# A list scheduler's order, tiled products and the conv half of the output projection inside the scan of a bidirectional RWKV-7 layer

## The chip, the cores and the metric

The kernel runs on one core of one Trainium2 chip. The metric is the device time of one execution in microseconds; a lower one is better. The times shown are three runs of the kernel before; the profile is one execution, recorded by the hardware profiler.

## What is computed

One layer of a bidirectional diffusion backbone, for 128 context tokens and 2048 latent tokens of width 1024. All is f32. Cut to what matters:

```python
h = rmsnorm(x) * (1 + scale) + shift
r, k, v, g_a, b_gate, c_gate, u_conv, g_b = split(h @ w_in)
r, k, v = token_shift(r, k, v)
ya = wkv(h, r, k, v, s0) * silu(g_a)          # 512 channels, 8 heads of 64, two directions
yb = b_gate * conv3(c_gate * u_conv) * silu(g_b)   # 512 channels
u = concat([ya, yb]) @ w_out
y = rmsnorm(x + gate * u) * final_g
# in wkv, per head and direction, for each token t:
S = S * w_t - (S @ kk_t) (kk_t * a_t)^T + v_t k_t^T
out_t = S @ r_t
```

## The kernel before

The work stands in three phases. **Phase 1** computes the norm, the input projection, the shifts, decays and the conv group, and spills them to DRAM scratch: `ops0` and `ops1` (four operands for each direction), `vt`, `sg`, `q`, and `mixT`, in whose rows 512 to 1023 the conv half `yb` lies when phase 1 ends. At its end `K.early()` begins the matrices of the first scan stages.

**Phase 2** is the scan in chunks of 64 tokens. It has 17 stages (`NST`). A stage handles a pair of heads (two heads of 64 make 128 rows) and eight chunks ("units") of each direction; stage 15 is the context, with all heads. What a stage s does, by the helper that issues it:

- `partL` loads the operands `rr` (512 KB a DMA, two for each direction); `partM` makes the matrices F and GA (`product`, L892): the operand is first copied by ACT into block-diagonal weights `bd` (`make_bd`, L779), a product uses all 128 rows and columns, DVE masks the result (L893). `transposes` makes Q (psQ, L885). The diagonal blocks of GA go to DRAM (`at`).
- `partI` runs on POOL: it loads the blocks as `ab`, inverts 32x32 triangles by substitution (L923 to L934) and stores `zt` (L935). `partM` and `partI` work on stage s+3 (`LA = 3`), in one of three slots.
- `partW` loads the stacked operands `stl`, `str` of stage s+1 (L843, L846), the values `sv` (L822), the inverse `zc` (L978); `partU` forms the inverse of 64x64 blocks from those of 32 by 32x32 products (psU L992, psW L999) into `zb`.
- `partB` makes X = F zb (L1018) and, from the stacked operands, E (L1029, masked by DVE at L1030).
- `partS` is the recurrence itself: for each of eight steps and each direction two products of E with `sv` (psS, L1054), whose upper 64 rows DVE scales into the next unit's `sv` (L1067); the lower rows are outputs, summed over directions in `y`.
- `finish` normalises a block of 512 tokens for a head pair (L1115 to L1137: square, reduce, root, scale, transposes psT L1132, gate), and stores it into `mixT` rows 0 to 511 (L1141).

All products of phase 2 are f32; the trace shows two matmul records for each.

The order of the work is written out by hand: `ORDER` and `MORD` say which piece of `partW`, `partU`, `partB` and `partM` is issued between which steps of `partS` (`main`, L1159 to L1225). Each engine works through its instructions in the order of issue; SP's queue issues nearly all DMAs.

**Phase 3** is the output projection with residual, gate and final norm, in 17 tiles of 128 tokens (`TILES`) and two column halves of 512. f32 operands are divided into two parts in f32r (`hi`, `lo`), and three products stand for one. A half of a tile needs 12 products with the attention rows (`psu<-..mha/mla`) and 12 with the conv rows (`..mhc/mlc`), L1287 to L1289. The first three tiles have their conv part done `ahead`, in stages 14 to 16 (psa); `tail` does the rest. A tile's result is multiplied by the gate (L1346), x is added (POOL, L1350), squared (L1351), scaled (L1356) and stored (L1357).

Of the kernel before, what the change touches and what calls it, by code (L numbers as in the profile page):

```python
# [672 lines left out]
SCR = {}  # L673
# [8 lines left out]
MORD = ("Ff", "GgD", "", "Q")  # L682
ON_DVE = ""
LA = 3


ORDER_END = ('LbbbL', 'UU', 'U', '', 'BBB', '', '', '', '')
ORDER = ('LbbbL', '', 'U', 'U', 'U', '', 'BBB', '', '')


def phase2(K):
# [6 lines left out]
    O.scaled = None  # L698

    def setup_first():  # L700
# [4 lines left out]
        O.pm = Pool(K, "p2m", "right", 2, PSUM)  # L705
# [15 lines left out]
        B.bd = ring(O.r1, 2, [128, 8, 128], "bd", zero)  # L721
        B.rr = ring(O.r1, 2, [128, 5, 8, 64], "rr", presetR)

    def new_slot(pool):
        i = len(B.slots)
        B.slots.append([tuple(pool.tile([128, 8, w], F32, tag=f"{n}{i}{d}", name=f"{n}{i}{d}", bufs=1) for n, w in (("F", 128), ("GA", 128), ("Q", 64))) for d in range(2)])

    def spare(i, name, dt):

        tags = ["F10", "GA10", "F11", "GA11", "F00", "F01", "GA00", "GA01"]  # L730
        if i >= 8:
            return O.rI.tile([128, 1024], dt, tag="ab", name=name, bufs=2)
        return O.r0.tile([128, 1024], dt, tag=tags[i], name=name, bufs=1)

    def setup_rest():
        O.l0 = Pool(K, "p2l0", "left")
        O.l1 = Pool(K, "p2l1", "left")
        O.p2 = Pool(K, "p2s", "left", 2, PSUM)
        O.pS = Pool(K, "p2S", "left", 4, PSUM)
# [13 lines left out]
        lt = ring(O.l1, 2, [128, 2, 8, 128], "stl", lambda t_: presetS(vl(t_)))  # L753
        rt = ring(O.l1, 2, [128, 2, 2, 8, 64], "str", presetS)
        B.lt, B.rt = lambda: vl(lt()), rt
        B.bu = O.l1.tile([128, 16, 32], F32, name="bu")
        B.zb = O.l1.tile([128, 2, 8, 128], F32, name="zb")
        zero(B.zb)

    def ring(pool, n, shape, name, init=None):  # L760
        l = [pool.tile(shape, F32, name=f"{name}{i}") for i in range(n)]
        if init:
            for t_ in l:
                init(t_)
        st = [0]

        def get():
            st[0] += 1
            return l[(st[0] - 1) % n]
        return get  # L770

    def copy(k, dst, src, negate=False):
        if negate:
            if k in ON_DVE:
                V.tensor_scalar(dst, src, -1.0, None, ALU.mult)
            else:
                P.activation(dst, src, AF.Copy, scale=-1.0)  # L777
        else:
            (V.tensor_copy if k in ON_DVE else P.copy)(dst, src)  # L779

    def zero(t_):
        G.memset(t_[:], 0.0)

    i2b = lambda n: B.I2[:].unsqueeze(1).broadcast_to((128, n, 64))

    def presetR(t_):
        V.tensor_copy(t_[:, 2], i2b(8))

    def vl(t_):
        return t_[:].rearrange("p h u (b t) -> p b h u t", b=2)  # L790

    def presetS(t_):
        for hd in range(2):
            V.tensor_copy(t_[0:64, 0, hd], B.I2[0:64].unsqueeze(1).broadcast_to((64, 8, 64)))

    def tl(shape, tag, b, pool=None, dt=F32):
        return (pool or O.l0).tile(shape, dt, tag=tag, name=f"{tag}_{K.u()}", bufs=b)

# [28 lines left out]
    H0, H1, FULL = slice(0, 64), slice(64, 128), slice(0, 128)  # L827
# [5 lines left out]
    def load_stk(t_, g, k, us):  # L833

        units = g.units[us]
        p, c0 = units[0]
        src = S[f"ops{g.d}"][k]
        n = 4 if p == units[-1][0] else 2
        for i in range(4 // n):
            dst = t_[0:64, 1, :, us.start + n * i:us.start + n * (i + 1)]  # L840
            x = src[(p + i) * 128:(p + i + 1) * 128, c0 * 64:(c0 + n) * 64]
            if t_ is g.rt:
# [5 lines left out]
    def half(g, n):  # L848

        h = n if g.d == 0 else 1 - n  # L850
        return slice(h * 4, h * 4 + 4)

    def partL(s):
        st = Ctx()
        st.g = []
        for gi, (d, units, blk) in enumerate(stages[s]):
            g = Ctx()
            st.g.append(g)
            g.d, g.units, g.blk = d, units, blk
            g.rr = B.rr()  # L860
            if blk is None:
                for i, k in ((0, 0), (1, 1), (3, 2), (4, 3)):
                    load(g.rr[:, i], d, k, units, FULL)
            else:
                p, c0 = units[0]
                src = S[f"ops{d}"][:, p * 128:(p + 1) * 128, c0 * 64:(c0 + 8) * 64]
                for i, k in ((0, 0), (3, 2)):
                    D(g.rr[:, i:i + 2].rearrange("p k u t -> p k (u t)"), src[k:k + 2].rearrange("k p t -> p k t"))
        return st

    def partM(s, st):

        at = S["at"][s]
        for gi, g in enumerate(st.g):
            d = g.d
# [28 lines left out]
            for piece in MORD:  # L904
                for c in piece:
                    ops[c]()
# [507 lines left out]
```

## Time and profile before

| | us |
|---|---|
| runs | 1751.56, 1760.31, 1761.01 |
| median | 1760.31 |
| span of the profiled execution, first to last instruction | 1752.9 |
| its PE busy | 1647.9 (94%) |
| its DVE, ACT, POOL busy | 1093.0, 870.1, 582.1 |
| first and last product of the recurrence (psS) | 1034.2, 1588.3 |
| last product of the tail | 1745.0 |

The profile gives the span of its execution and no other time for it; the median of the runs lies 7.4 us above that span, the lowest run 1.3 us below. PE is TensorE's matmuls, PEld its weight loads, DVE VectorE, ACT ScalarE, POOL GpSimd, SP the queue that issues DMAs. `L1054` is a line of the kernel. In a row of the timeline stand the start, the length, the engine, the line, the operation, output and inputs, and in the end how many records were merged; in brackets is the idle time ahead of it and what ended it. Matmuls overlap in the records, so that the time from one start to the next says what one costs, not its length. A row of groups gives busy time and mean length in ns.

### The profile page before, as it was taken

The page shows a single profiled execution, that of the slowest core. Times are in us where ns is not written, and L with a number is a line of the kernel's source. Part 1 is how long each engine was busy: PE and PEld are TensorE (multiplying, and loading weights), DVE is VectorE, ACT ScalarE, POOL GpSimd, SP SyncE. Part 2 cuts the span into 40 slices and gives each one's busy share as a digit, 9 for nine tenths or more (in the row PEclk, how much of TensorE's full clock was granted, in tenths as well). Part 3 has the DMA queues.
Part 4 walks back from the last instruction along what each step waited for, and adds up shares of the span by engine and source line. Part 5 has one row for each costly group of instructions (what it writes and reads, how often), then busy time and mean ns, then how long its engine had stood idle before and what let it go on. Part 6 is the DMA issues. An engine that isn't in the chain of part 4 may idle for free. (4 is left out here: it accounts for less than half of the span.)

```text
span 1752.9 us, 33041 instructions
## 1 busy us (share of the span) xinstructions
PE 1647.9 (94%) x12400; PEld 1558.8 (89%) x12400; DVE 1093.0 (62%) x2092; ACT 870.1 (50%) x1719; POOL 582.1 (33%) x1089
## 2 busy tenths in 40 slices
PE   5999899998999999999998989999999999899998
PEld 2889898998999998999998979899999999787886
DVE  5875788866567766567764544475776666656333
ACT  4534455534143433334442367687788787633222
POOL 0011111111011101011120587777777778223221
PEclk9899999999999999999999998899999999999999
DMA  9797778785557646477666585587677875746442
GB/s 367 208 234 220 233 241 246 232 255 151 148 160 227 169 147 174 135 258 217 195 214 225 173 196 135 141 192 187 174 198 189 191 185 120 180 151 206 151 144 90
DMA packets 315825, 335.69 MB, mean 192 GB/s; under 512 B 166985, under 2 KB 263881, under 8 KB 301585
## 3 DMA queue, kind: packets, MB, share of 16 engines
q1 hardware_dynamic: 243360, 324.52, 62.6%
q10 hardware_dynamic: 70944, 4.60, 2.9%
q0 software_dynamic: 1360, 4.46, 0.7%
q8 instruction: 98, 1.61, 0.4%
q14 instruction: 63, 0.51, 0.1%
HBM read 221.42 MB, written 112.08 MB: 190 GB/s over the span
## 5 line engine op out<-in xcount | busy, mean ns | idle before, releaser
L934 POOL TENSOR_TENSOR zt<-zt,ztmp 128x30 f32<-128x30 f32 (+7 forms) x510 | 197.3, 387 | 39.3
L1054 PE MATMUL psS<-sv,E 128*128 128x64 f32 x1088 | 155.1, 277 | 1.0 <-DVE sv L1067 0.6
L1029 PE MATMUL psE<-str,stl 128*128 128x128 f32 x1088 | 144.1, 281 | 11.3 <-DVE E L1030 7.0
L1054 PEld LDWEIGHTS psS<-sv,E 128*128 128x128 f32 x1088 | 145.4, 200 | 3.3 <-DVE sv L1067 0.8
L1029 PEld LDWEIGHTS psE<-str,stl 128*128 128x128 f32 x1088 | 131.8, 194 | 14.1 <-DVE E L1030 7.9
L931 POOL TENSOR_TENSOR ztmp<-ab,zt 128x60 f32<-128x60 f32 (+7 forms) x255 | 130.8, 513 | 19.2
L1067 DVE TENSOR_TENSOR sv<-psS,pc 64x128 f32<-64x128 f32 x254 | 69.2, 277 | 92.9 <-PE psS L1054 92.2
L779 ACT COPY bd<-rr 64x512 f32<-64x512 f32 x136 | 84.0, 617 | 75.7 <-DMA rr<-scr_ops 23.3
L323 POOL TENSOR_TENSOR shk<-rawl 128x384 f32<-128x384 f32 (+1 forms) x24 | 20.7, 861 | 291.9 <-ACT rawl L319 291.9
L1030 DVE TENSOR_TENSOR E<-psE,msk 128x512 f32<-128x512 f32 x136 | 92.7, 684 | 33.0 <-PE psE L1029 32.3
L892 PE MATMUL psF<-rr,bd 128*128 128x128 f32 x544 | 80.0, 295 | 16.2 <-ACT Q L779 9.8
L892 PEld LDWEIGHTS psF<-rr,bd 128*128 128x128 f32 x544 | 70.7, 203 | 20.4 <-ACT Q L779 12.9
L1350 POOL TENSOR_TENSOR z<-z,x 128x512 f32<-128x512 f32 x32 | 43.6, 1364 | 126.6 <-DVE z L1346 105.9
L1018 PE MATMUL psX<-F,zb 128*128 128x128 f32 x544 | 78.2, 297 | 3.2 <-ACT zb L777 2.3
L197 POOL TENSOR_TENSOR hslb<-kd,hshb 128x384 fp32r<-128x384 f32 (+1 forms) x24 | 26.7, 1113 | 164.0 <-ACT hshb L196 143.5
L160 PE MATMUL mmc<-h,w 128*128 128x384 f32 (+1 forms) x192 | 67.9, 354 | 13.4 <-ACT q1r L321 9.8
L323 POOL TENSOR_TENSOR shv<-rawl 128x384 f32<-128x384 f32 (+1 forms) x24 | 25.4, 1060 | 153.4 <-ACT rawl L319 153.4
L892 PE MATMUL psG<-rr,bd 128*128 128x128 f32 x544 | 72.0, 280 | 4.4 <-DVE F L893 4.4
L1018 PEld LDWEIGHTS psX<-F,zb 128*128 128x128 f32 x544 | 71.6, 209 | 4.0 <-POOL zt L934 1.9
L892 PEld LDWEIGHTS psG<-rr,bd 128*128 128x128 f32 x544 | 65.7, 193 | 5.0 <-DVE F L893 4.8
L161 PE MATMUL mmc<-h,w 128*128 128x384 f32 (+1 forms) x192 | 66.1, 344 | 0.0
L162 PE MATMUL mmc<-h,w 128*128 128x384 f32 (+1 forms) x192 | 65.7, 342 | 0.0
(307 smaller groups left out, 5205.4 us busy)
## 6 DMA issues: line engine op xcount, KB each, us to landing
w<-scr_wsp SPq DMA_DIRECT2D x68, 1024.0 KB, 7.3
scr_wsp<-w SPq DMA_DIRECT2D x34, 1024.0 KB, 6.0
rr<-scr_ops SPq DMA_DIRECT2D x64, 512.0 KB, 4.6
scr_ops<-sp SPq DMA_DIRECT2D x160, 192.0 KB, 5.2
wr<-in_win SPq DMA_DIRECT2D x34, 512.0 KB, 6.3
ab<-scr_at SPq DMA_DIRECT2D x34, 256.0 KB, 4.2
x<-in_x SPq DMA_DIRECT2D x17, 512.0 KB, 3.8
wadas<-in_wada SPq DMA_DIRECT2D x8, 1024.0 KB, 13.0
```

The costliest lines, as they stand in the source:

```text
L160: T.matmul(ps[:, :n], w[:, 0, k], hh[:, 0, k, :n], start=k == 0, stop=False)
L161: T.matmul(ps[:, :n], w[:, 0, k], hh[:, 1, k, :n], start=False, stop=False)
L162: T.matmul(ps[:, :n], w[:, 1, k], hh[:, 0, k, :n], start=False, stop=k == 7)
L779: (V.tensor_copy if k in ON_DVE else P.copy)(dst, src)
L892: T.matmul(ps[:, i, :].rearrange("p (a b) -> p a b", b=64), w[:, u, :], x[:, :, u, :], start=True, stop=True)
L931: G.tensor_tensor(tv, ab[:, j:j + 2, j + 2:32].unsqueeze(1).broadcast_to((128, kn, 2, n)), zt[:, :kn, j:j + 2].unsqueeze(3).broadcast_to(( ...
L934: G.tensor_tensor(zt[:, :kn, j + 2:32], zt[:, :kn, j + 2:32], tv[:, :, r], ALU.subtract)
L1018: T.matmul(px[:, i, :], B.zb[:, gi, us.start + i, :], g.F[:, us.start + i, :], start=True, stop=True)
L1029: T.matmul(pe[:, i, hd, :].rearrange("p (b t) -> p b t", b=2), g.lt[:, :, hd, us.start + k + i].rearrange("p b t -> p (b t)"), g.rt[:, :, ...
L1030: V.tensor_tensor(g.E[n][:, k:k + 2].rearrange("p a b c -> p (a b) c"), pe[:].rearrange("p a b c -> p (a b) c"), B.msk[:, ME[g.d]].unsquee ...
L1054: T.matmul(sp[gi][:, q, hd, :], g.E[n][:, k, hd, :], sv[:, u, hd, :], start=True, stop=True)
L1067: r = V.tensor_tensor(dst, sp[gi][0:64, q], B.pc[0:64, d, 2 * p:2 * p + 2, c:c + 1].broadcast_to((64, 2, 64)), ALU.mult)
```

## The change

1. **Order.** `ORDER`, `MORD` and the generators go. `record` now enters each instruction or small group as an operation of a `Plan`: engine, a cost in ns, a lag until its result is there, buffers read and written, PSUM banks, the tile shape, a due time. `Plan.order` simulates the engines and picks at each point the operation that can start first, by due time among those ready; on PE another tile shape counts as 1200 ns later (`TURN`) and costs 95 (`SWITCH`). The operations are then issued in the order of their simulated start, on PE, DVE, ACT, POOL and SP (`manual_schedule`).
2. **Tiles.** F, G and X are made of 64x64 products ("quarters"); the block-diagonal copies `bd` go. S and E are made of products of 128 rows and 64 columns ("halves"). Q is no longer made from `rr`: the operand `be` is loaded a second time and transposed where it is used (`queries`).
3. **Buffers.** `rr`, `stl`, `str`, `E`, `held` have one buffer for each direction (or direction and half); the output of `finish` is written over `sg`. PSUM has 2 banks for `m`, 2 for `s`, 3 for S, 1 for the filler.
4. **Conv half.** `filler` computes gate * (conv part) + x for each of 34 halves of tiles in the scan's stages 0 to 15, 12 products each, and stores it in a scratch `zx`. `tail` has 12 products for a half, and adds `zx` where it added x. It begins when the planned part is issued.

The core of the diff:

```diff
-MORD = ("Ff", "GgD", "", "Q")
-ORDER = ('LbbbL', '', 'U', 'U', 'U', '', 'BBB', '', '')
+PERIOD = 28000
+EARLY = 4
+SWITCH = 95
+TURN = 1200
+HOP = 50
+FULL, HALVES, QUARTERS, SMALL = range(4)
...
+    def order(self):
+        for o in reversed(self.ops):
+            for d in o.deps:
+                d.due = min(d.due, o.due - d.ns - d.lag - HOP)
...
+                t0 = min(t for t, _ in at)
+                o = min((o for t, o in at if t <= t0), key=lambda o: (o.due + (TURN if e == "PE" and o.mode != mode else 0), o.n))
+                if best is None or t0 < best[0]:
+                    best = t0, o
...
+        return sorted(done, key=lambda o: (o.start, o.n))
...
-    def make_bd(t_, src):
-        copy("b", t_[0:64, :, 64:128], src[0:64])
-        copy("c", t_[64:128, :, 0:64], src[64:128])
+    def place(u, hd):
+        return hd if u < 4 else 1 - hd
...
+    def product(s, d, banks, w, x):
+        for i in range(4):
+            for m in range(2):
+                for hd in range(2):
+                    u, r = m * 4 + i, rows64(hd)
+                    T.matmul(four(banks[m])[rows64(place(u, hd)), i, :].rearrange("p (a b) -> p a b", b=64), w[r, u, :], x[r, :, u, :], start=True, stop=True)
...
+    def product_X(s, n, banks):
+        for i in range(4):
+            for d in range(2):
+                u = half(d, n).start + i
+                for r in range(2):
+                    T.matmul(four(banks[d])[rows64(r if d == 0 else 1 - r), i, :], B.zb[rows64(r), d, u, :], slot(s, d)[0][rows64(r), u, :], start=True, stop=True)
+    def product_E(d, n, k, b):
...
+        for i in range(2):
+            for hd in range(2):
+                for x, c in enumerate((H0, H1)):
+                    u = half(d, n).start + k + i
+                    T.matmul(pe[c, i, hd, :].rearrange("p (b t) -> p b t", b=2), B.lt[d][:, x, hd, u], B.rt[d][:, :, hd, u], start=True, stop=True)
+    def queries(d, n, b):
+        for k in range(2):
+            u = half(d, n).start + 2 * k
+            T.transpose(four(b)[:, k, :], B.be[d][:, u:u + 2, :].rearrange("p u t -> p (u t)"), B.idt[:])
...
+        with tc.manual_schedule(engines={E.PE, E.DVE, E.Activation, E.Pool, E.SP}):
+            for o in plan.order():
...
+                o.fn(*use)
+        O.lf.close()
+        O.l1.close()
+        tail = K.tail()
+        for _ in range(1 + EARLY):
+            next(tail)
+        O.p2.close()
+        K.rest(tail)
...
+            add("POOL", lambda: invert(s), 24500, r=[("ab", s % 2, 0), ("ab", s % 2, 1)], w=[("ztd", s)], lag=3900)
...
+                def step(b, d=d, n=n, k=k, q=q, sv=sv, u=u):
+                    for hd in range(2):
+                        for x in (H0, H1):
+                            T.matmul(sums(b)[x, q, hd, :], B.E[d][n][:, k, hd, x], sv[:, u, hd, :], start=True, stop=True)
...
+            add("SP", lambda: fetch("sg", B.sg), 400, w=[("sg",)], lag=3700)
...
+            add("SP", lambda: fetch("q", B.w), 600, w=[("w",)], lag=3700)
...
+            add("DVE", lambda: V.tensor_tensor(B.sg[:], B.sg[:], B.w[:], ALU.add), 600, r=[("w",)], w=[("sg",)], lag=70)
+            add("SP", store, 400, r=[("sg",)], w=[("mix", p, blk)], lag=2700, due=due + 6000)
...
+        def quad(n, i, due):
...
+            add("SP", fetch, 400, w=[("fraw",)], lag=3400)
+            add("SP", lambda: D(x[:], A["x"][i * 128:i * 128 + 128, cs]), 400, w=[("fx",)], lag=3300)
+            divided(lambda: q.raw, lambda: m[:], lambda: q.ml, [("fraw",)], [("fm",)], [("fraw",)], due)
...
+                def chunk(b, k=k):
+                    ms = third(m[:]), third(q.ml)
+                    T.matmul(b[:], ms[0][:, k], w[0][:, k], start=k == 0, stop=False)
+                    T.matmul(b[:], ms[0][:, k], w[1][:, k], start=False, stop=False)
+                    T.matmul(b[:], ms[1][:, k], w[0][:, k], start=False, stop=k == 3)
...
+            add("DVE", lambda b: V.tensor_tensor(z[:], b[:], gt[:], ALU.mult), 610, r=[("fps",), ("fg",)], w=[("fz",)], use=first, lag=70)
+            add("DVE", lambda: V.tensor_tensor(z[:], z[:], x[:], ALU.add), 600, r=[("fx",)], w=[("fz",)], lag=70)
+            add("SP", lambda: D(S["zx"][i * 128:i * 128 + 128, cs], z[:]), 400, r=[("fz",)], lag=2700)
...
-            D(xt[:], A["x"][t0:t0 + 128, :])
+            D(xt[:], S["zx"][t0:t0 + 128, :])
...
-                if mc:
-                    products(ps, mc, cs, CONV, True, False)
-                products(ps, ma, cs, ATT, not mc, True)
...
+                products(ps, ms, [(wk[k][0][:, cs], wk[k][1][:, cs]) for k in range(4)])
+                V.tensor_tensor(z[:, cs], ps[:], gb[:, s, cs], ALU.mult)
```

More of the change, by code (lines that the diff above doesn't have):

```diff
@@ L704, in setup_first @@
         O.r1 = Pool(K, "p2r1", "right")
-        O.pm = Pool(K, "p2m", "right", 2, PSUM)
+        O.pm = Pool(K, "p2m", "right", 1, PSUM)
+        B.pm = [O.pm.tile([128, 512], F32, name=f"psm{i}") for i in range(2)]
         B.msk = O.r0.tile([128, 4, 128], F32, name="msk")
@@ L846, in load_stk, with half @@
                     D(dst[:, hd], x[hd * 64:hd * 64 + 64].rearrange("c (u t) -> c u t", t=64))
-    def half(g, n):
-        h = n if g.d == 0 else 1 - n
+    def half(d, n):
+        h = n if d == 0 else 1 - n
         return slice(h * 4, h * 4 + 4)
[L853 to L869, printed above, removed]
```

854 lines of the change are left out of this document (456 added, 398 removed).

## The prediction

> **What bounds the kernel now.** I read the page's head, then the table by stretch for the middle of the scan and for the tail. Columns: stretch and length, busy time of PE, PEld, DVE, ACT, POOL with instruction counts, granted clock, share of the DMA engines, GB/s.
>
> ```profile
> span 1752.9 us, 33041 instructions
> ...
> 1088.11:1465.94 377.83, 364.77 (x4357) 354.83 (x4357) 240.39 (x492) 300.36 (x574) 284.35 (x639) 0.97 0.74 179
> 1588.30:1745.04 156.74, 156.49 (x685) 127.12 (x683) 69.61 (x113) 41.54 (x104) 38.73 (x29) 1.00 0.43 148
> ```
>
> PE is busy 97% of the scan's stretch and all of the tail; no other engine passes 80%. The timeline of PE places the stages (start, length, operation, records):
>
> ```profile
> 1034.22 0.56 PE L1054 MATMUL psS<-sv,E 128*128 128x64 f32 x4
> ...
> 1088.11 1.20 PE L992 MATMUL psU<-zr,GA 32*32 32x32 f32 x64
> ...
> 1211.69 2.00 PE L892 MATMUL psG<-rr,bd 128*128 128x128 f32 x16
> 1213.53 1.95 PE L1029 MATMUL psE<-str,stl 128*128 128x128 f32 x16
> 1215.32 1.00 PE L1054 MATMUL psS<-sv,E 128*128 128x64 f32 x8
> 1216.16 0.61 PE L885 MATMUL psQ<-idt,rr 128*128 128x128 f32 x4
> 1216.60 1.06 PE L892 MATMUL psF<-rr,bd 128*128 128x128 f32 x8
> 1217.59 1.20 PE L992 MATMUL psU<-zr,GA 32*32 32x32 f32 x64
> 1218.72 1.10 PE L1054 MATMUL psS<-sv,E 128*128 128x64 f32 x8
> ...
> 1465.94 1.20 PE L992 MATMUL psU<-zr,GA 32*32 32x32 f32 x64
> ...
> 1588.30 0.56 PE L1054 MATMUL psS<-sv,E 128*128 128x64 f32 x4
> ...
> 1745.04 0.39 PE L1289 MATMUL psu<-woh,mla 128*128 128x512 f32 x1
> ```
>
> The first and last psU rows lie twelve stages apart: 377.83/12 = **31.5 us a stage**. The scan runs from 1034.2 to 1588.3, the tail's matmuls to 1745.0, and 7.9 us follow. From start to start a matmul record costs: E 1.79/16 = 0.112 us, G 0.115, S 0.84/8 = 0.105, Q 0.11, psU 1.13/64 = 0.018. Every f32 product makes two records. A stage has 64 of E, 64 of S, 96 of F, G and X (X taken like F), 8 of Q, 128 of U and W, 4 of T: 7.2 + 6.7 + 10.9 + 0.9 + 2.3 + 0.4 = 28.4 us, 29.3 at clock 0.97, and (377.83 - 364.77)/12 = 1.1 us idle: 30.4 of 31.5. A tail record costs 156.74/685 = 0.229 us.
>
> POOL is nearly as tight. Rows: it hands over one inverse (L935) and the next; then a wait for its input:
>
> ```profile
> 1133.41 0.61 POOL L935 DMA_DIRECT2D scr_zt<-zt  x1 [0.30 <-POOL zt L934]
> ...
> 1160.74 0.58 POOL L935 DMA_DIRECT2D scr_zt<-zt  x1 [0.30 <-POOL zt L934]
> ...
> 1291.82 0.20 POOL L923 COPY dgp<-ab 128x16 f32<-128x16 f32 x1 [2.94 <-DMA ab<-scr_at]
> ```
>
> An inverse without a wait takes **27.3 us**. So a stage can't fall far below 28, whatever PE saves.
>
> **The change part by part, per stage.** *Quarters* (F, G, X): 16 products for each kind and direction, in 64x64 tiles, take the place of 8 full-width ones whose weights were half zeros; at two records each that is 192 records for the 96 of now. They stream the same 128 columns. If four tiles overlap, 192 records at 0.112/4: 5.4 us instead of 10.9. The trace shows no 64-row tile. The nearest row is psU: two 32x32 tiles, 0.018 a record, where a quarter of E's stream would be 0.028 one after the other; so different tiles do overlap, 1.6-fold of 2. Bounds: 5.4 (four), 10.8 (two), 21.5 (none). I take 5.4, because psU's 0.018 also leaves room for four records in 0.112. *Halves* (S, E): twice the products at half width. E: 128 records at 0.056 if two overlap, 7.2, no gain; none overlapping, 14.3. S: streams 64 columns, half of E's, so 0.028 to 0.030 in pairs: 3.8 instead of 6.7; alone, 7.2. I take the pairs, by psU again. *Shape changes*: psF's 8 records before psU took 0.99 against 0.90, so 0.09 a change. Four now; I count 24 (eight rounds of S, each between other shapes): +1.8 (bounds 0.5 and 4). *Queries* replace psQ at the same 8 records. *Conv half*: 34 halves of 12 records at 0.229 = 93.4 us, in 16 stages 5.8 us each.
>
> PE: 7.2 + 3.8 + 5.4 + 2.3 + 0.9 + 0.4 + 5.8 + 2.2 = **28.0 us**; at clock 0.97 and with 1.1 idle, **30.0**.
>
> *Around PE.* Groups of the scan's stretch (busy us, mean ns), and a POOL pair beside a DVE operation with two SBUF inputs, and the same pair free of one:
>
> ```profile
> L779 ACT COPY bd<-rr 64x512 f32<-64x512 f32 x94 | 58.0, 617 | 29.3 <-issue 9.2 <-PE psG L892 4.7 <-PE psS L1054 3.2
> L779 ACT COPY Q<-psQ 128x512 f32<-128x512 f32 x24 | 14.0, 585 | 0.6
> L1030 DVE TENSOR_TENSOR E<-psE,msk 128x512 f32<-128x512 f32 x96 | 65.5, 684 | 14.8 <-PE psE L1029 14.6
> L1137 DVE TENSOR_TENSOR yo<-yo,w 128x512 f32<-128x512 f32 x10 | 7.8, 776 | 0.0
> ...
> 1296.12 0.56 POOL L934 TENSOR_TENSOR zt<-zt,ztmp 128x30 f32<-128x30 f32 x2
> ...
> 1325.66 0.93 POOL L934 TENSOR_TENSOR zt<-zt,ztmp 128x30 f32<-128x30 f32 x2
> ...
> 1325.80 0.68 DVE L1122 TENSOR_TENSOR y<-y,yss 128x512 f32<-128x512 f32 x1
> ```
>
> ACT: 300.36/12 = 25.0, less bd 4.8 and Q 1.2, plus 2.25 casts at 0.6: 20.4. DVE: 20.0, plus per stage 2.25 differences and 2.1 adds from SBUF (0.78) and 2.1 products from PSUM (0.68): 24.8, 82% of 30. Neither binds, but S's scaling now queues behind more. POOL: 27.3 plus 4.4 two-input DVE operations, each of which cost a pair 0.37 above: **28.9**. [...]
>
> DMA: 0.74 x 31.5 = 23.3 us a stage now, 242 GB/s at full share. Added: 2.1 x 768 KB for the conv half (mixT, x, zx), 512 KB because `be` is loaded a second time, some weights: 2.25 MB. Its rows are 512 to 2048 bytes like the tail's, where 148/0.43 = 344 GB/s: 6.5 us. Sum **29.8**, which only fits if the queue hardly rests. The bounds of the added part are 6.2 (nothing but its bytes, faster) and 9.3 (the scan's rate).
>
> So three floors, 30.0, 28.9 and 29.8, come close together. They are of different engines and need not meet, but each waits for the others through single buffers; I take 30.3 for stages 0 to 13 (bounds 28.3, POOL and a wait of 1, and 33). Against 31.5 the scan itself hardly gains: what PE saves with quarters and S (8.4 us), the conv half (5.8) and the shape changes (1.8) take back. What is late next after PE's products is the load of operands: lt, rt, be and zb have one buffer, where they had two or stood in rr. Stages 14 and 15 have no F, G or inverse: 28.0 - 3.6 plus waits, 25.5 each. Stage 16 is the chain of its eight steps, 13.
>
> *The handover.* SP's queue is in the planned order, so the tail's loads stand behind the last `mixT` store. Two blocks finish in stage 16 and share the single buffers sg and w. Landing times (us) and an issue:
>
> ```profile
> w<-scr_q SPq DMA_DIRECT2D x11, 256.0 KB, 4.3
> sg<-scr_sg SPq DMA_DIRECT2D x10, 256.0 KB, 3.9
> scr_mixT<-yo SPq DMA_DIRECT2D x10, 256.0 KB, 2.7
> mxa<-scr_mixT SPq DMA_DIRECT2D x12, 256.0 KB, 2.9
> ...
> 1293.05 0.61 SPq L1141 DMA_DIRECT2D scr_mixT<-yo  x1
> ```
>
> Copy, square, reduce (three passes at 0.68), q (4.3), add, store (2.7), the second sg (3.9), two passes, store issue, three issues at 0.6, mx (2.9), two passes, and issues between: 23 us (bounds: 8 if only one block's chain counts, 26). In it nothing is left for PE. Before, L1132's transposes and the tail's products stood mixed, and the conv half of a tile needed no finished block: that cover is gone.
>
> *The tail*: 34 halves of 12 records at 0.229: 93.4 us, and 7.9 behind. Tile time falls from 11.0 to 5.5, DVE there from 69.61/156.74 x 11.0 = 4.9 to about 4, so PE still leads.
>
> **Sum.** The start stays at 1034.2: phase 1 isn't touched, and the first stages' products only get shorter (bounds 1030 and 1040). 1034.2 + 14 x 30.3 + 51 + 13 + 23 + 93.4 + 7.9 = 1646.7 of span. The median shown, 1760.3, stands 7.4 above the span of the profile; I add it: **1654 us**. In general 1229.9 + 14 P, with P the time of a stage.
>
> **Rivals.**
> 1. *Thin stages.* POOL's waits shrink, DMA packs better, P = 28.3 (POOL's 27.3 plus 1): 1626; with a short handover 1611. For: all of ACT's block copies go. Against: the DMA sum.
> 2. *Quarters overlap by two only.* PE 33.4, P about 35.5 at the same clock and idle: 1727. For: the nearest row shows two tiles, not four. [...]
> 3. *A stiff order.* The order is fixed from costs in the code, and each engine keeps to it. It counts 24.5 us for an inverse that takes 27.3, 3.2 to 4.6 for landings that get longer at full share, and a POOL that is free at the plan's start, although the inverse of stage 1 is handed over only after the first S:
>
> ```profile
> 1038.52 0.60 POOL L935 DMA_DIRECT2D scr_zt<-zt  x1 [0.31 <-POOL zt L934]
> ```
>
> So the loads of zc stand too early in SP's queue, and one that waits holds the operand loads behind it. Price: the 2.94 wait above once or twice a stage, P = 33 to 35: 1692 to 1720.
> 4. *Slower: tiles do not overlap.* Then each product of half the width takes the array as long as one of the full width, and there are twice as many. Place: every E, S, F, G and X. Price: E 14.3, S 7.2, F, G and X 21.5, the rest 11.6: 54.6 us, P = 57.4, 2033. It decides from P = 37.9 (1760.3), that is when the tiled products take (37.9 - 1.1) x 0.97 - 11.6 = 24 us instead of 16.4. Against: psU, which overlaps.
>
> That the change doesn't do what it says would show as conv records left in the tail; the code leaves none.
>
> **Chances.** Forecast (1640 to 1690) 0.53, rival 1 0.18, rival 2 0.11, rival 3 0.10, rival 4 0.08. The range 1605 to 1715 takes in the forecast, rival 1 and about half of 2 and 3. About 0.5% is what a measurement of this kernel can tell from no change: faster 0.90 (all but rival 4 and a stray end of 3), same 0.02, slower 0.08.
>
> **What would show it.** Right: psU rows about 30 us apart, DMA share over 0.9 and DVE at 0.8 in the scan, PE records of the quarters at 0.03 and of the halves at 0.03 to 0.06, a gap of some 20 us on PE before the first psu, and a tail of 94 us at 0.229 a record. Wrong: quarters at 0.056 (rival 2) or 0.11 (rival 4); POOL waiting for ab over 4 us a stage (rival 3); psu records with gaps, which would mean that the tail has another bound, z's or x's two buffers first.

## The result, and the profile after

The changed kernel takes **1784.78 us** (median of 4 runs, 1780.79 to 1796.02) beside 1760.4 for the kernel before on the same chip: ratio **1.0145**, 95% interval 1.0097 to 1.0193. It is slower; 1654 was forecast. The chips of the experiments below run the kernel before in 1739 to 1746 us, so times are compared there as ratios and scans by their length. On one of them the changed kernel was timed again (e19): ratio 1.0165 (1.012 to 1.0209).

The head of the page, and the table by stretch (columns as in the prediction) for 14 stages of the scan and for the tail:

```profile
span 1778.7 us, 40744 instructions
...
1061.99:1589.81 527.82, 463.85 (x8596) 368.00 (x8592) 333.09 (x669) 282.71 (x567) 365.02 (x766) 0.92 0.81 215
1667.00:1766.30 99.30, 98.44 (x411) 78.34 (x412) 67.67 (x101) 36.33 (x96) 47.03 (x32) 0.97 0.66 213
```

PE's timeline places the stages. The U product (line 997; `zr,GA`) is what the prediction calls psU:

```profile
1033.12 0.45 PE L1185 MATMUL psS<-sv,E 128*64 128x64 f32 x8 [2.35 <-issue]
...
1061.99 1.20 PE L997 MATMUL pss<-zr,GA 32*32 32x32 f32 x64
...
1589.81 1.20 PE L997 MATMUL pss<-zr,GA 32*32 32x32 f32 x64
...
1659.89 0.45 PE L1185 MATMUL psS<-sv,E 128*64 128x64 f32 x8 [0.31 <-DVE sv L1206]
...
1666.96 0.79 PE L1365 MATMUL psu<-woh,mh 128*128 128x512 f32 x1 [2.55 <-ACT mh L1359]
...
1766.44 0.40 PE L1367 MATMUL psu<-woh,ml 128*128 128x512 f32 x1
```

A stage takes 527.82/14 = **37.7 us**, where 31.5 was the time before and 30.3 the forecast. The first table splits it: PE busy at full clock 463.85 x 0.92 / 14 = 30.5, lost to the clock 463.85 x 0.08 / 14 = 2.7, PE idle (527.82 - 463.85)/14 = 4.6. The kernel before, by the same sum from its row in the prediction, has 29.5, 0.9 and 1.1. So PE's work per stage grew by only 1.0 us, although 5.8 us of the tail (by the forecast) moved into it; the stage is longer mostly because PE **stands** more and gets **less clock**. A stretch of 28 us shows both side by side. Six rows of PE's timeline, then the table in steps of 4 us:

```profile
1310.84 1.10 PE L935 MATMUL psm<-rr 64*64 64x128 f32 x32
...
1319.78 0.38 PE L1022 MATMUL psm<-idt,be 128*128 128x128 f32 x2
1322.23 1.20 PE L997 MATMUL pss<-zr,GA 32*32 32x32 f32 x64 [2.07 <-DVE E L1165]
...
1330.96 2.75 PE L935 MATMUL psm<-rr 64*64 64x128 f32 x32 [0.84 <-ACT str L1139]
1335.11 1.98 PE L935 MATMUL psm<-rr 64*64 64x128 f32 x32 [1.39 <-DVE F L938]
...
1339.19 1.97 PE L1009 MATMUL pss<-F,zb 64*64 64x128 f32 x28 [1.69 <-DVE sg L1269]
```

```profile
1320.00:1324.00 4.00, 1.93 (x82) 1.64 (x80) 2.96 (x6) 3.07 (x6) 3.45 (x8) 0.98 1.04 362
1324.00:1328.00 4.00, 3.24 (x66) 2.49 (x65) 2.67 (x6) 3.31 (x8) 3.37 (x9) 0.50 1.04 293
1328.00:1332.00 4.00, 2.90 (x24) 2.03 (x27) 1.31 (x2) 3.20 (x7) 3.53 (x7) 0.50 1.02 262
1332.00:1336.00 4.00, 2.61 (x44) 2.21 (x44) 1.98 (x3) 2.04 (x4) 3.48 (x7) 0.50 1.11 250
1336.00:1340.00 4.00, 2.31 (x44) 1.91 (x40) 1.61 (x3) 0.00 (x0) 3.50 (x7) 0.50 1.07 280
1340.00:1344.00 4.00, 4.00 (x47) 2.92 (x43) 2.61 (x4) 3.73 (x7) 3.45 (x8) 0.50 0.54 198
1344.00:1348.00 4.00, 4.00 (x73) 3.17 (x71) 3.39 (x6) 0.80 (x2) 2.66 (x9) 0.96 0.50 151
```

PE stands for 2.07 us, until DVE has masked E; from 1324 on the granted clock is 0.50, and it stays there for 20 us, in which PE has gaps of 0.8 to 1.7 us. From 1340 to 1344 PE is busy without a gap, and in the next window the clock is 0.96. The group of 32 quarters that took 1.10 us takes 1.98 and 2.75 in those 20 us. Here the standing and half the clock come together. They don't everywhere: some 30 us later PE stands longer, and the clock of the four windows from 1356 on is 1.00, 1.00, 1.00 and 0.53, the last after a second gap, of 1.60 us, at 1365.9:

```profile
1355.85 0.69 PE L1185 MATMUL psS<-sv,E 128*64 128x64 f32 x16 [2.45 <-DVE sv L1206]
...
1367.51 1.44 PE L997 MATMUL pss<-zr,GA 32*32 32x32 f32 x64 [1.60 <-DVE zr L1112]
```

Last the sign that the prediction named for rival 3, POOL's waits in 1060:1500 (sum, number, longest in us), of the changed kernel and of the one before. It is there: 106.6 us in 440/37.7 = 11.7 stages are 9.1 a stage, where over 4 were named.

```profile
POOL dgp L967 <- DMA ab<-scr_at: 106.6, 10, 28.1
```

```profile
POOL dgp L923 <- DMA ab<-scr_at: 32.8, 11, 7.6
```

### The profile page after: what moved, and what is told of

Read it like the earlier page. It is cut to its first block, busy times and chain, and to the rows that moved or that the text cites. A ratio compares the mean times of both kernels' runs of the same rounds, so it can differ in the third digit from the quotient of the medians.

```text
span 1778.7 us, 40744 instructions
## 1 busy us (share of the span) xinstructions
PE 1586.1 (89%) x16208; PEld 1416.5 (80%) x16208; DVE 1142.3 (64%) x2183; ACT 769.2 (43%) x1568; POOL 602.0 (34%) x1083
## 5 line engine op out<-in xcount | busy, mean ns | idle before, releaser
L1017 PE MATMUL pss<-str,stl 128*64 128x128 f32 x2176 | 145.3, 283 | 15.0 <-ACT str L1159 10.5
L1017 PEld LDWEIGHTS pss<-str,stl 128*64 128x64 f32 x2176 | 123.3, 142 | 26.4 <-ACT str L1159 15.6
L1185 PEld LDWEIGHTS psS<-sv,E 128*64 128x64 f32 x2176 | 84.8, 143 | 55.7 <-DVE sv L1206 20.9
L1185 PE MATMUL psS<-sv,E 128*64 128x64 f32 x2176 | 105.8, 235 | 21.5 <-DVE sv L1206 12.4
L1165 DVE TENSOR_TENSOR E<-pss,msk 128x512 f32<-128x512 f32 x136 | 91.4, 681 | 22.7 <-PE pss L1017 17.6
L935 PE MATMUL psm<-rr 64*64 64x128 f32 x2176 | 84.8, 295 | 20.0 <-DMA rr<-scr_ops 8.8
L935 PEld LDWEIGHTS psm<-rr 64*64 64x64 f32 x2176 | 67.2, 145 | 36.0 <-issue 18.2
L1412 PE MATMUL psf<-fwh,fm 128*128 128x512 f32 x136 | 71.6, 526 | 12.1 <-ACT fm L1383 12.1
L938 DVE TENSOR_TENSOR F<-psm,msk 128x512 f32<-128x512 f32 x68 | 44.5, 682 | 33.8 <-PE psm L935 33.7
L160 PE MATMUL mmgb<-h,w 128*128 128x384 f32 (+1 forms) x192 | 64.4, 335 | 0.0
L161 PE MATMUL mmgb<-h,w 128*128 128x384 f32 (+1 forms) x192 | 64.2, 334 | 0.0
```

The source lines that it names most:

```text
L160: T.matmul(ps[:, :n], w[:, 0, k], hh[:, 0, k, :n], start=k == 0, stop=False)
L161: T.matmul(ps[:, :n], w[:, 0, k], hh[:, 1, k, :n], start=False, stop=False)
L935: T.matmul(four(banks[m])[rows64(place(u, hd)), i, :].rearrange("p (a b) -> p a b", b=64), w[r, u, :], x[r, :, u, :], start=True, stop=True)
L938: V.tensor_tensor(dst[:, m * 4:m * 4 + 4, :], four(bank), mask.unsqueeze(1).broadcast_to((128, 4, 128)), ALU.mult)
L1017: T.matmul(pe[c, i, hd, :].rearrange("p (b t) -> p b t", b=2), B.lt[d][:, x, hd, u], B.rt[d][:, :, hd, u], start=True, stop=True)
L1165: after(o, add("DVE", lambda b, d=d, k=k: V.tensor_tensor(B.E[d][n][:, k:k + 2].rearrange("p a b c -> p (a b) c"), b[:].rearrange("p (a c) ...
```

## The experiments

The first runs test four theories. **A**: the order is stiff, made from wrong numbers. **B**: the conv half's transfers lengthen the input of the inverse. **C**: the conv half's work on PE, DVE and ACT is in the way. **D**: the single buffer `dg`. The measure is the scan, first to last psS row, since phase 1 varies by 20 us between runs and chips (first psS row at 1011.5 in e15, 1033.1 in the changed kernel); the kernel before has 554. Clock, PE's idle time and POOL's wait for ab are those of 1060:1500 (440 us). Only e17, e19 and e20 were timed several times in alternation with the kernel before ("in rounds"), the others once. Three kernels were profiled twice; their scans differ by 0.6, 6.6 and 2.2 us (changed kernel and e19, e8 and e20, e13 and e17), so a difference of a few us says nothing.

| run | scan us | clock | PE idle | ab wait | time, before beside it |
|---|---|---|---|---|---|
| changed kernel | 626.8 | 0.91 | 54.7 | 106.6 | 1784.8, 1760.4 |
| e19 changed kernel again | 627.4 | 0.91 | 58.3 | 91.2 | 1768.8, 1742.2 |
| e1 POOL's numbers | 639.0 | 0.89 | 54.7 | 88.6 | 1780.2, 1739.6 |
| e14 landings | 624.6 | 0.92 | 51.4 | 73.7 | 1762.8, 1745.6 |
| e8 landings and POOL | 598.2 | 0.95 | 48.1 | 63.7 | 1739.5, 1739.4 |
| e20 the same, in rounds | 591.6 | 0.97 | 47.7 | 61.5 | 1737.7, 1742.2 |
| e11 landings x 2.0 and POOL | 596.2 | 0.95 | 51.8 | 73.1 | 1744.9, 1745.6 |
| e12 shared DMA and POOL | 616.1 | 0.94 | 54.0 | 115.9 | 1751.4, 1745.6 |
| e18 a number that should not matter | 629.4 | 0.93 | 66.9 | 75.7 | 1760.2, 1741.8 |
| e6 two `dg` | 642.1 | 0.91 | 61.4 | 100.6 | 1768.7, 1739.4 |
| e10 conv transfers issued by ACT | 643.3 | 0.89 | 58.7 | 79.0 | 1778.0, 1739.4 |
| e2 no conv half | 519.2 | 0.89 | 75.0 | 34.2 | 1668.1, 1739.6 |
| e16 no conv half, landings and POOL | 528.1 | 0.89 | 77.4 | 33.1 | 1665.9, 1741.8 |
| e4 conv transfers only | 590.6 | 0.82 | 108.9 | 76.0 | 1738.4, 1739.6 |
| e3 conv engines only | 597.7 | 0.91 | 41.2 | 64.8 | 1734.8, 1739.6 |
| e15 conv products only | 570.7 | 0.96 | 32.1 | 49.7 | 1700.6, 1741.8 |
| e9 half of the conv halves | 555.8 | 0.93 | 58.5 | 43.0 | 1689.4, 1739.4 |
| e13 half in the scan, half in the tail | 542.5 | 0.94 | 50.9 | 43.1 | 1729.0, 1745.6 |
| e17 the same, in rounds | 540.3 | 0.94 | 48.6 | 40.9 | 1726.7, 1741.8 |

**e1, POOL's numbers in the order**

```diff
-            add("POOL", lambda: invert(s), 24500, r=[("ab", s % 2, 0), ("ab", s % 2, 1)], w=[("ztd", s)], lag=3900)
+            add("POOL", lambda: invert(s), 27400, r=[("ab", s % 2, 0), ("ab", s % 2, 1)], w=[("ztd", s)], lag=3900)
...
+        add("POOL", lambda: None, 26000, w=[("ztd", 1)], lag=3900)
         blocks(0)
```

> Only two entries of the order are changed: an inverse is counted at 27.4 us instead of 24.5, and POOL is counted as busy for the first 26 us of the plan (the inverse of stage 1, which it really still works on). The changed kernel has 37.7 us a stage (first to last psU row, 14 intervals) and the rest of it gives total = 1257 + 14 P. Theory A (a stiff order made from wrong costs of POOL): the waits of POOL for ab (126 us over 12 inverses) fall below 50, P 32 to 34, time 1705 to 1735. Theory B (the transfers of the conv half lengthen the landings in the input chain of the inverse) and theory C (the conv half's work on PE, DVE and ACT stands in the way): P within 1 of 37.7, time 1770 to 1800. Theory D (the single dg buffer between two stores): the same as B and C.

639.0 us: theory A in this form falls. POOL waits less for ab (88.6 instead of 106.6) and the scan is no shorter, so that wait alone does not set it.

**e2, no conv half**

```diff
-            while at[0] < len(quads) and at[0] < len(quads) * (s + 1) / (NST - 1):
+            while False and at[0] < len(quads) * (s + 1) / (NST - 1):
...
-            D(xt[:], S["zx"][t0:t0 + 128, :])
+            D(xt[:], A["x"][t0:t0 + 128, :])
```

> The conv half is left out altogether (its loads, casts, products and stores; the tail adds x in place of zx, so the output lacks the conv half). Theory A: the order's waits stay, because they come from the costs of POOL and of the landings; P 34 to 37, time 1735 to 1775. Theory B and theory C alike: the stage falls to what POOL and PE need without it, P 29 to 31, time 1665 to 1690. Theory D: the dg buffer is as single as before, P 34 to 37.

519.2 us and 1668.1, the time that B and C said; the stage, over the same 14 intervals as above, is (1491.0 - 1033.8)/14 = 32.7 us, where they said 29 to 31. The conv half costs 626.8 - 519.2 = **108 us** in the scan, more than the 93.4 that its products take where they flow (the tail). And the scan without it is not 448 us, which the prediction's own terms would give (14 x 28.3, POOL's 27.3 plus 1; 51 less 12 for the conv half in stages 14 and 15; 13 for the last). The stretch 1060:1500:

```profile
1060.00:1500.00 440.00, 365.03 (x8168) 315.44 (x8168) 268.79 (x573) 260.23 (x532) 346.54 (x762) 0.89 0.77 197
```

PE stands for 75 of 440 us and has a clock of 0.89; the gaps that the conv half was to fill were there. POOL's rows show where a part of the excess arises:

```profile
1025.52 0.58 POOL L979 DMA_DIRECT2D scr_zt<-zt  x1 [0.31 <-POOL zt L978]
...
1048.96 0.20 POOL L967 COPY dgp<-ab 128x16 f32<-128x16 f32 x1 [22.86 <-DMA ab<-scr_at]
...
1074.94 0.60 POOL L979 DMA_DIRECT2D scr_zt<-zt  x1 [0.30 <-POOL zt L978]
...
1503.98 0.60 POOL L979 DMA_DIRECT2D scr_zt<-zt  x1 [0.30 <-POOL zt L978]
```

POOL's third inverse waits 22.86 us for its input at the start of the scan (2.59 in the kernel before), and the 14 handovers after it come 429.0/14 = 30.6 us apart, not 28.3. What makes these inputs late was not tested.

**e3 and e4, one side of the conv half each**

First e3 (it computes with the gate tile in place of what was loaded), then e4 (there the casts, differences, products, multiplication and addition go, x is stored, and the loads of the conv half's weights go too):

```diff
-            add("SP", fetch, 400, w=[("fraw",)], lag=3400)
-            add("SP", lambda: D(x[:], A["x"][i * 128:i * 128 + 128, cs]), 400, w=[("fx",)], lag=3300)
-            divided(lambda: q.raw, lambda: m[:], lambda: q.ml, [("fraw",)], [("fm",)], [("fraw",)], due)
...
+            divided(lambda: gt[:], lambda: m[:], lambda: q.ml, [("fg",)], [("fm",)], [("fraw",)], due)
...
-            add("SP", lambda: D(S["zx"][i * 128:i * 128 + 128, cs], z[:]), 400, r=[("fz",)], lag=2700)
```

```diff
-            divided(lambda: q.raw, lambda: m[:], lambda: q.ml, [("fraw",)], [("fm",)], [("fraw",)], due)
...
-            add("SP", lambda: D(S["zx"][i * 128:i * 128 + 128, cs], z[:]), 400, r=[("fz",)], lag=2700)
+            add("SP", lambda: D(S["zx"][i * 128:i * 128 + 128, cs], x[:]), 400, r=[("fx",)], lag=2700)
```

> The conv half's work on PE, DVE and ACT stays, its loads of mixT and x and its store of zx for each tile are left out (it computes with the gate tile in their place, and the tail adds x, so the output lacks the conv half). Theory B (transfers): P 30 to 33, time 1675 to 1720, landings of the at store back from 7.6 to about 5 us. Theory C (engine work): P 36 to 38, time 1760 to 1790. Theory A: P 35 to 37.5. If both parts matter, P lies between 33 and 36.

> The complement of the run before it: the conv half's loads of mixT, x and gate and its stores to zx stay, its casts, differences, products and adds are left out (the stored tile is x, so the output lacks the conv half). Theory B (transfers): P 35 to 38, time 1745 to 1790. Theory C (engine work): P 29 to 32, time 1665 to 1705. Theory A: P 35 to 37.

597.7 and 590.6: the engines' work alone costs 78.5, the transfers alone 71.4, both 107.6 and not 149.9. Neither B nor C is it alone, and what they cost overlaps. In e4 PE has the least to do and the worst clock:

```profile
1060.00:1500.00 440.00, 331.12 (x7006) 290.15 (x7002) 237.90 (x500) 219.03 (x449) 307.88 (x680) 0.82 0.89 237
```

**e15, only the conv half's products on PE**: no loads for each tile, one constant operand, no casts, differences, products with the gate, adds or stores.

> Of the conv half only PE's products stay, on one constant tile (no loads for each tile, no casts, differences, products, adds or stores; the tail adds x, so the output lacks the conv half). Scan without any of it 519 us, with all of its engines' work 598. Theory H (the gaps cost twice: PE stands, and then gets half the clock for some us; products that wait for nothing fill the gaps): scan 515 to 545, less time lost to the clock than without them although PE has 93 us more to do. Theory C (PE's products themselves stand ahead of the chain that sets the stage): scan 565 to 600. Then the casts and adds on ACT and DVE would be nearly free.

```profile
1060.00:1500.00 440.00, 407.88 (x8163) 337.53 (x8163) 263.26 (x550) 249.80 (x508) 323.06 (x714) 0.96 0.74 192
```

570.7: 34 x 12 records, 93.4 us at the tail's rate, cost 51.5. The length lies in theory C's range, the clock as H said: idle falls from 75.0 to 32.1 us, and the clock rises from 0.89 to 0.96. Added in this order, PE's products cost 52 us, the casts and adds around them another 27 (e3; theory C had them nearly free), the transfers the last 29. Since costs overlap, another order would divide them otherwise: alone, the transfers cost 71.

**e9, half of the conv halves**

```diff
-        quads = [(n, i) for n in range(2) for i in ["w0", "w1"] + list(range(1, 17)) + [0]]
+        quads = [(n, i) for n in range(1) for i in ["w0", "w1"] + list(range(1, 17)) + [0]]
...
```

> Only the first 17 of the 34 conv halves, spread over the same stages; the other 17 are left out and the tail adds x (the output lacks the conv half). The scan is 519 us with none and 627 with all. Theory of a floor (POOL sets the stage until the conv half's work on PE and DMA has filled their slack): the first half is nearly free, scan 525 to 550, time 1675 to 1700. Theory of a chain (each conv half costs its own time because it stands in queues that the stage waits for): in proportion, scan 565 to 580, time 1710 to 1735.

555.8: the first 17 halves cost 37 us, the next 17 another 71. This lies between the two expectations, and is bent as the floor theory says. That POOL is the floor is not shown.

**e6, two `dg` buffers, and three `z` in the tail**

```diff
-        B.dg = O.rI.tile([128, 8, 32], F32, name="dg")
+        B.dg = [O.rI.tile([128, 8, 32], F32, name=f"dg{i}") for i in range(2)]
...
-            z = tl([128, 1024], "z", i)
+            z = tl([128, 1024], "z", i, b=3)
```

> Two edits that can be read apart, since one acts in the scan and one in the tail. Scan (first to last psS row; 627 us in the changed kernel, 519 without the conv half): dg has a buffer for each direction, so that the second extraction no longer waits for the first one's store. Theory D (the single dg buffer holds ACT, DVE and with them the states): the waits of ACT and DVE for dg go, 2 to 4 us a stage, scan 570 to 600. If dg is only one of many places where an engine stands: scan 615 to 635. Tail (psu rows, 99 us): z has three buffers instead of two. If z's buffers bound the tail, it falls to 93 to 95 us; if another chain does, it stays at 98 to 100.

A third change is part of this run: the two buffers `so` of the context's states are made one. Scan 642.1: theory D falls. The tail's psu rows run from 1660.52 to 1757.83, 97.3 us instead of 99.5, and 9.1 us follow instead of 12.3: z's buffers were worth about 5 us, of the 10.5 that the tail and its end miss. In e18, with the old buffers, the rows take 98.0, so the 2 us are near what varies by itself; the end of all runs with the old buffers and the whole conv half in the scan, 12.2 to 13.4, is clear of 9.1.

**e10, the conv half's transfers issued by ACT** (Q is ACT's DMA start)

```diff
...
-            add("SP", fetch, 400, w=[("fraw",)], lag=3400)
+            add("ACT", fetch, 400, w=[("fraw",)], lag=3400)
...
-            add("SP", lambda: D(x[:], A["x"][i * 128:i * 128 + 128, cs]), 400, w=[("fx",)], lag=3300)
+            add("ACT", lambda: Q(x[:], A["x"][i * 128:i * 128 + 128, cs]), 400, w=[("fx",)], lag=3300)
...
-            add("SP", lambda: D(S["zx"][i * 128:i * 128 + 128, cs], z[:]), 400, r=[("fz",)], lag=2700)
+            add("ACT", lambda: Q(S["zx"][i * 128:i * 128 + 128, cs], z[:]), 400, r=[("fz",)], lag=2700)
```

> The conv half's loads and its store are issued by ACT instead of SP; bytes, engines' work and buffers stay. Theory G (head of the line: a conv load that waits for its single buffer holds the operand loads, the ab and the zc behind it on SP): scan 570 to 605 us, POOL's wait for ab below 70 us in 1060:1500. Theory B in the form that the bytes themselves cost, or theory C: scan 615 to 640. If ACT takes over the waiting and passes it on to the copies behind it: above 640.

643.3: no gain, and above 640 as the last case of the expectation says. Either SP's head of line isn't the cause, or ACT passes the same waits on; this run can't tell the two apart.

**e8, e14, e11, e12: the order's other numbers**

First e14; e8 is this with e1's edits, e11 the same as e8 with a factor of 2.0. The at store is lengthened by both lines: 5.0 x 1.45 = 7.25 us (10 in e11), and not the 5.0 that the expectation names; in the changed kernel's trace (1060:1500) it lands after 4.3 us in the median, the loads of ab after 5.0 and of rr after 5.7, for which e8 plans 5.4 and 6.2. Then e12, which has e1's edits too:

```diff
+        o.lag = int(lag * 1.45) if lag >= 2000 else lag
...
-                add("ACT", lambda d=d: diag_store(s, d), 80, r=[("dg",)], w=[("at", s, d)], lag=3600)
+                add("ACT", lambda d=d: diag_store(s, d), 80, r=[("dg",)], w=[("at", s, d)], lag=5000)
```

```diff
+            if o.lag >= 2000 and o.eng != "POOL":
+                b = max(t + o.ns, free.get("DMA", 0.0))
+                free["DMA"] = b + {4300: 2000, 3200: 500, 3600: 500}.get(o.lag, 1000)
+                o.end = b + o.lag
```

> The order is planned with landings 1.45 times as long (the at store at 5.0 us, and so on, nearer to the 4 to 6 us of the trace), and with the inverse at 27.4 and POOL busy at the start as in the first run. Theory A in its second form (the order is stiff because it counts on landings that are too short): POOL's wait for ab below 60 us in 1060:1500, scan 570 to 600 us, time 1720 to 1755. If the order's numbers are not the cause: scan 610 to 650, time 1765 to 1800.

> The order is planned with landings 1.45 times as long, but with the inverse at 24.5 and POOL free at the start, as in the changed kernel. Both numbers of POOL and the landings together brought the scan from 627 to 598 us; those of POOL alone gave 639. If the landings are what the order has wrong: scan 585 to 612. If only both together help: 618 to 640. POOL's wait for ab in 1060:1500 follows: near 64 us in the first case, near 100 in the second.

> As the run with landings 1.45 times as long and POOL's own costs, but with a factor of 2.0. Theory of the stiff order, with contention beyond the median landing: more slack helps further, scan 565 to 592. If 1.45 has taken what there is and longer landings only push the loads so early that they hold buffers: 595 to 640.

> The order's landings stay short, but the planner counts the DMA engines as one shared resource: each transfer of SP or ACT takes its turn on it for 0.5, 1 or 2 us (128, 256, 512 KB at about 260 GB/s, which is 218 GB/s over a share of 0.83 in the changed kernel's scan), and the inverse and POOL's start are as in the first run. By this plan a stage takes 33 to 34 us instead of 31. If the order is wrong because it knows no contention: scan 565 to 600, as good as or better than with longer landings. If uniform slack is what helps: 605 to 640.

598.2 with both corrections, 624.6 with the landings alone, 639.0 with POOL alone (e1): only **together** do they help. A factor of 2.0 does the same (596.2), so what the runs show is the worth of landings long enough in the plan, not of exact ones. Counting the shared DMA engines gives less (616.1). POOL's wait for ab was 115.9 us in e12 and 75.7 in e18, whose scan is longer: that wait alone doesn't tell the length of the scan.

**e16, the same corrections without the conv half**

> No conv half (left out as in the second run), with the order planned on landings 1.45 times as long, the inverse at 27.4 and POOL busy at the start. If the order's wrong numbers cost in the scan as such: 485 to 506 us instead of 519, that is 29 to 30 us a stage, near POOL's 27.3 and a wait. If they only hurt where the conv half fills the queues: 510 to 530.

528.1 beside 519.2: without the conv half correcting the numbers gains nothing.

**e18 and e19, how far chance goes**

For e18:

```diff
-HOP = 50
+HOP = 60
```

> The changed kernel with one number of the planner moved that should not matter: 60 ns instead of 50 between an operation and what depends on it. It gives another order of the same work. Theory of the stiff order: the scan's time depends on how the fixed order happens to meet the real durations, so it moves by 5 to 20 us from 627, to either side. If the order is good enough for such details: 622 to 632.

> The changed kernel as it is, on the chip of the experiments. If the scan depends on the order and not on the chip: 620 to 635 us again, ratio to the kernel before 1.008 to 1.020. If the experiments' chip is what shortened the scan of the corrected order: 595 to 610, ratio 0.998 to 1.004.

629.4 and 627.4. With e1, e6, e10 and e14 the orders without both corrections lie between 624.6 and 643.3, those with them between 591.6 and 598.2 (e12, with POOL's numbers and another count of the transfers, has 616.1). The chip doesn't make the difference.

**e20, the corrected order (e8) in rounds**

> The changed kernel with the corrected numbers of the order alone (landings 1.45 times as long, the inverse at 27.4, POOL busy at the start), now in rounds. Theory of the stiff order: scan 590 to 605 again, ratio to the kernel before 0.995 to 1.004, some 1.5% below the changed kernel. If it was chance: scan 615 to 640, ratio above 1.008.

Ratio to the kernel before **0.9982** (0.9954 to 1.001), beside 1.0165 for the changed kernel on the same chip. The stretch:

```profile
1060.00:1500.00 440.00, 392.33 (x7566) 310.82 (x7560) 300.34 (x594) 246.21 (x494) 316.55 (x662) 0.97 0.88 232
```

The order's numbers are worth as much as the whole loss against the kernel before; with longer ones no difference is left that the interval could tell. PE stands nearly as long as in the changed kernel (47.7 of 440 us instead of 54.7), but has a clock of 0.97 instead of 0.91: most of the gain is clock.

**e13 and e17, half of the conv halves in the scan, half in the tail** (nothing left out; corrected order)

```diff
-        quads = [(n, i) for n in range(2) for i in ["w0", "w1"] + list(range(1, 17)) + [0]]
+        quads = [(n, i) for n in range(2) for i in ["w0", "w1"] + (list(range(1, 17)) + [0] if n == 0 else [])]
...
-                products(ps, ms, [(wk[k][0][:, cs], wk[k][1][:, cs]) for k in range(4)])
+                products(ps, ms, [(wk[k][0][:, cs], wk[k][1][:, cs]) for k in range(4)] + [(O.wc[0][:, k], O.wc[1][:, k]) for k in range(4) if n])
...
```

> Nothing is left out: the conv half of the first 512 columns in the scan (17 halves), that of the other 512 in the tail, whose second half of each tile has 24 instead of 12 records; landings and POOL in the order as in the run with 1.45. Theory of a floor (the first halves are cheap in the scan, the later ones dear): scan 535 to 560, tail 99 + 17 x 12 x 0.229 = 146 us (140 to 150), time 1710 to 1738, faster than both kernels. Theory of a chain (each half costs the same in the scan): scan 555 to 580, time 1735 to 1760.

> The half and half version again (17 conv halves in the scan, 17 in the tail, corrected numbers of the order), now timed in rounds beside the kernel before. One look gave 1729 beside 1746: ratio 0.985 to 0.996 if that holds. The chip and the clock move single runs by about 1%, so a ratio of 1.00 would say that it was chance.

Scan 542.5 and 540.3, tail 154.1 and 150.8 us (psu rows from 1561.47 to 1712.27 in e17; 140 to 150 was expected), ratio to the kernel before **0.9916** (0.9891 to 0.9942): faster than both kernels. Beside e16, which has the same corrections and no conv half, the first 17 halves cost the scan 540.3 - 528.1 = 12 us. Beside e20 the scan is 51 us shorter and the psu rows 50 longer (150.8 instead of 100.5): the second 17 cost as much in the one place as in the other. So what e17 gains against the kernel before comes from the first 17. Against e20 its profile is shorter by 5.6 us at the end (7.8 behind the last psu row instead of 13.4) and 4 us at the start, which this edit was not meant to change.

## Why the prediction was wrong

The span forecast was 1646.7, the span is 1778.7. By its terms, in us: start -1.1, scan 626.8 instead of 488.2 (**+138.6**), handover 7.1 instead of 23 (-15.9), psu rows 99.5 instead of 93.4 (+6.1), end 12.3 instead of 7.9 (+4.4).

*The tiles: right.* Start to start on PE's timeline:

```profile
1309.94 0.50 PE L1412 MATMUL psf<-fwh,fm 128*128 128x512 f32 x1
1310.28 0.39 PE L1413 MATMUL psf<-fwl,fm 128*128 128x512 f32 x1
1310.51 0.40 PE L1414 MATMUL psf<-fwh,fraw 128*128 128x512 f32 x1
1310.84 1.10 PE L935 MATMUL psm<-rr 64*64 64x128 f32 x32
1311.87 1.97 PE L1017 MATMUL pss<-str,stl 128*64 128x128 f32 x32
1313.77 0.50 PE L1412 MATMUL psf<-fwh,fm 128*128 128x512 f32 x1
...
1314.66 0.69 PE L1185 MATMUL psS<-sv,E 128*64 128x64 f32 x16
1315.28 0.50 PE L1412 MATMUL psf<-fwh,fm 128*128 128x512 f32 x1
```

32 quarters take 1.03 us (0.032 each: 3.5 of them in the 0.112 of one full-width record before), 32 of E's halves 1.90 (0.059 each: 1.9 in 0.112), 16 of S's 0.62 (0.039 with the change of shape). Rivals 2 and 4 fall with these rows.

*PE's work: 28.0 forecast, 30.5 measured.* The term most mis-sized is the conv half. The tail's 0.229 a record holds where records flow; in the scan three stand between other shapes and take 0.90 (1309.94 to 1310.84), 0.30 each: 8.5 such chunks a stage are 7.7 instead of 5.8. By these rows E is 7.6 (7.2 forecast), S 5.0 (3.8) and the quarters 6.2 (5.4); with 3.6 for U, W, Q and T this makes 30.1, and the 2.2 that the forecast adds for changes of shape stand inside the rows.

*POOL and DMA: near.* POOL's busy time is 365.02/14 = 26.1 us a stage, 2.4 more than the 284.35/12 before, where 1.6 was added. The DMA share of 0.81 of 37.7 is 30.5 us a stage (29.8 forecast).

*"Three floors ... I take 30.3": this step failed.* It carried the clock of 0.97 and the 1.1 us of idle over from a kernel whose PE was busy for 97% of the time, to one whose PE is busy for 88% (463.85 of 527.82), more than any other engine. Measured: clock 0.92, idle 4.6. Of the 7.4 us that a stage takes more than forecast, 2.5 are PE's work, 1.8 the clock and 3.2 PE's standing (4.6 instead of 1.1 and the 0.3). The prediction itself wrote that the floors belong to different engines and that each waits for the others, and then added 0.3 us for it.

*Rival 3 named a part of the cause, at a chance of 0.10, and had its path wrong.* The numbers that it called wrong in the order are those that e20 corrects. But it let the loads of zc wait at the head of SP's queue, and they wait less than in the kernel before (1060:1500, changed kernel and before):

```profile
SPq L1110 <- DMA scr_zt<-zt: 8.8, 5, 4.6
```

```profile
SPq L978 <- DMA scr_zt<-zt: 40.3, 10, 9.2
```

By which waits the wrong numbers cost their time is open. The runs put the scan's +138.6 together like this: without the conv half the scan is 519 instead of 448 (+71), and the conv half costs 108 where the forecast has 488 - 448 = 40 (+68). Of these 68 the wrong numbers of the order are 35 (626.8 to 591.6; e20 beside the changed kernel), shown by the run. The longer chunks, 1.9 us in 16 stages, would be about the other 30; that is argued, and e15 speaks against a plain sum, because there the products alone add only 51.5 to the scan. The +71 is **open**: it isn't the order's numbers (e16), and PE's waits there are spread over many pairs (the largest has 8.1 of 75 us). If POOL's handovers set the pace of e2's scan, the late third inverse (21 us behind 28.3) and 14 x 2.3 would be some 53 of it; no run tests that. More buffers for lt, rt or zb weren't tried.

*The handover: wrong, in favour.* The first of the tail's loads stands ahead of the last two stores of `mixT` in SP's queue:

```profile
1658.85 0.43 SPq L1463 DMA_DIRECT2D mx<-scr_mixT  x1
...
1662.68 0.46 SPq L1246 DMA_DIRECT2D w<-scr_q  x1
...
1671.68 0.33 SPq L1275 DMA_DIRECT2D scr_mixT<-sg  x1
...
1680.69 0.32 SPq L1275 DMA_DIRECT2D scr_mixT<-sg  x1
```

The first tail product runs at 1666.96, before both stores, and needs neither block; so the 23 us chain never stood between scan and tail.

*The tail.* 408 records at 0.229 are 93.4 us at full clock; the granted 0.97 makes it 96.3, and z's buffers perhaps 2 more (e6). The 4.4 us more at the end, which the forecast carried over as 7.9, are in good part z's buffers too (9.1 in e6).

## What to carry to other kernels

An engine that was busy for 97% of the time had little idle time (1.1 us a stage) and nearly full clock (0.97); when a change lets it idle (here 4.6 us, at a clock of 0.92), neither the old idle time nor the old clock may be carried over. Work moved into its gaps is worth only what finds free time there: here the first 17 halves cost the scan 12 us and the next 17 cost 51, as much as in the tail. A planned order needs durations that the kernel which runs it keeps to: lengthen all that its trace shows to be too short, together, and judge by the end time, not by the one wait that looks worst.

## What the runs showed of the hardware

The granted clock of PE is 0.50 to 0.53, or 0.96 and more, in the windows of 4 us that are shown above. After a gap of 2.07 us that ends at 1322.23 it was 0.50 from 1324 to 1344; gaps of 0.8 to 1.7 us, with PE busy for 58 to 81% of each 4 us (1324 to 1340), came with it. A gap of 2.45 us at 1353.4 was not followed by it, one of 1.60 at 1365.9 was; no run shows what decides. Over 440 us (1060:1500) the mean clock follows the idle time only in part: 0.82 with 109 us idle (e4), 0.89 with 75 (e2), 0.96 with 32 (e15), but 0.97 with 48 (e20) and 0.91 with 41 (e3). So in these runs the sum of the gaps doesn't settle the clock; how they lie was not worked out.
